# A two-layer hybrid trunk: three more engines keep the program's order

## The chip, the cores and the metric

The kernel runs on one core of a Trainium2 chip. The metric is the device time of the program in microseconds (us), the median of 3 runs of the kernel before: 746.13 (745.88 to 746.42).

## The reference

The kernel computes a decoder trunk of two layers over a residual stream of 1024 features, 16 learned meta tokens and then 256 real ones. All data are float32.

- Layer 0 normalises (RMSNorm) and multiplies by one input matrix whose columns are split over two mixers. *Sparse attention*, 8 heads of 64: a small indexer scores every key for every query, the 64 best keys are kept (the meta tokens always), then softmax with a relative-position bias. *Retention*, 4 heads (128 for query and key, 256 for value): rotary positions, scores times a decay, a group norm and a swish gate. Both outputs go through one output matrix and are added to the stream.
- Layer 1 has *stick-breaking attention*, 16 heads of 64: with z the score of an earlier key, its weight is exp(log sigmoid(z) + sum of log sigmoid(-z') over the keys between). An output matrix and the addition follow.
- After each mixer comes a gated MLP of 2816 hidden features: up and gate projections, a causal convolution of width 3 over the gate, silu(gate) times up, a down projection, the addition. A last RMSNorm ends it.

```
z = einsum(q, k) * scale
log_1m = where(mask, log_sigmoid(-z), 0)
rest = cumsum(log_1m, reverse) - log_1m
a = where(mask, exp(log_sigmoid(z) + rest), 0)
out = einsum(a, v)
```

## The kernel before, in words

**Data.** Features lie on the partitions, the 272 tokens on the free axis. Every weight matrix is cut into 128 x 128 tiles, read once and in one order, as a stream of chunks of 16 tiles (1 MB). `Stream` (from L89) holds three such chunks (`raw`), and splits each half chunk of eight tiles into two parts in the type fp32r: ScalarE copies `hi` (L122), VectorE subtracts it from `raw` to get `lo` (L126). Activations are split likewise (`xh` and `xl`, `ah` and `al`, `oh` and `ol`). A product is then three matmuls: high by high, low by high, high by low (L197 to L199).

**Order on TensorE.** `project` runs jobs one after the other; a job is a group of 8 to 22 tile products into one PSUM bank, and an evacuation on the other engines. `get`, called before each tile, makes `lo` two halves ahead of the tile in use and `hi` three halves ahead; four halves are kept. Everything else that TensorE does (scores, transposes, attention products) stands in coroutines that `Sched.tick` moves on by one step, every four tile products (L199 and after). A coroutine issues its step's instructions on all engines and then yields a number of ticks, which are fixed by hand (`D0` to `D6`, `AV`, `RS`, `PT`, `TK`, `VT`, `VC`).

**Order on the other engines.** The context is opened with a planner that simulates a time line and orders each engine's instructions by it. L76 takes TensorE out of that: it keeps the program's order throughout. The start (from L338) and the first norm are inside narrower blocks that pin ScalarE and VectorE, in the first also GpSimd. Everywhere else the planner orders ScalarE, VectorE, GpSimd and SyncE, and SyncE issues the weight loads.

**Layer 0's mixer.** `indexer` fills `sc` and `drop` with zeros, adds the relu scores, runs six rounds of max and match_replace (L451, L453) and writes `drop` (L459). `dsa` takes pairs of heads: `bm` = `drop` minus bias on GpSimd (L524), scores (L530, L531), minimum on VectorE (L534), exponential on ScalarE (L537), normalise (L543, L545), transposes (L551 to L554), their copies `ptk` (ScalarE) and `ptm` (VectorE, L557), products with the values (L566 to L571). `dsa_meta` does the meta tokens' own rows: a memset of `pf` (L581), the scores of 16 x 16 (L587) with an evacuation into `pf`, softmax, transposes, `pts` (L606), products (L612). `ev_rot` evacuates a rotary query or key into `qb` or `kb`, with the last addition on GpSimd (L642). `ret` transposes values (L671 to L673), scales and centres them as `vb` (L680, L687), and multiplies them with the scores (L696 to L698). There are three banks of pool "a" for all this, and three for projections.

**Feed-forward.** `ev_g` evacuates a gate group and starts `c` on ScalarE (L911); a tick later come two VectorE passes and silu, and `ev_u` gives `u`. 22 pairs of groups in each layer.

**Layer 1's stick-breaking.** Jobs run q, k for eight pairs of heads, and v three pairs later. `ev_q` makes `qc` and its parts, `ev_k` the parts `kd` and `kl` of the keys. `stick` then goes in steps: scores (L1069, L1070) and their copies `zs`; absolute value (L1075), exponential (L1077), logarithm (L1078); max-add into `sp` (L85) and masks on GpSimd (L1014); addition of 16 rows, parts `sh` (L1086) and `sl` (L82); the cumulative sums as products (L1093 to L1101), each subtracted from `zs`; exponential (L1104) and masks; products with `vt` (L1117 to L1121), `oh` (L1122) and `ol`. `v_t` transposes `vv` and copies it into `vt` (L1055). Two buffers of most tiles, four banks of pool "a", one of "o".

Of the kernel before, what the change touches and what calls it, by code (L numbers as in the profile page):

```python
# [65 lines left out]
def trunk(ctx, tc, hT, wp, gains, gng, convw, convb, relb, oneh, cosT, sinT, decay, gfin, out):  # L66
# [6 lines left out]
    tmp = ctx.enter_context(tc.tile_pool(name="tmp", bufs=2))  # L73
    pp = ctx.enter_context(tc.tile_pool(name="pp", bufs=3, space=PSUM))
    dram = ctx.enter_context(tc.tile_pool(name="dram", bufs=1, space=DRAM))
    ctx.enter_context(tc.manual_schedule(engines={mybir.EngineType.PE}))  # L76

    def log_exp():
        tc.keep_in_program_order(S.preload_act_table_set("natural_log_exp_and_others"))
# [1157 lines left out]
```

## Time and profile before

| | us |
|---|---|
| median of 3 runs | 746.13 (745.88 to 746.42) |
| profiled execution | 745.54 |
| its span, first to last instruction | 743.5 |
| mean granted TensorE clock, share of full speed | 0.997 |
| TensorE busy in the span | 726.9 |
| VectorE, ScalarE, GpSimd busy | 538.4, 420.8, 87.8 |

One profiled execution is read; its span leaves out 2.0 us around the program's own instructions. The chain that ended last, followed back from the last instruction, gives 88% of the span to TensorE, 5% to VectorE, 2% each to ScalarE and GpSimd. To place the stages in time: layer 0's first `c` of the feed-forward (L911) starts at 224.2 us, the first `qs` copy of the stick-breaking layer (L1024) at 424.0, its last `oh` (L1122) at 527.0, and layer 1's last `c` at 670.6.

### The profile page before, as it was taken

What the parts mean: (1) busy time and instruction counts of PE and PEld (TensorE: products, weight loads), DVE (VectorE), ACT (ScalarE), POOL (GpSimd) and SP (SyncE); (2) the same over time, 40 slices, a digit from 0 to 9 for tenths busy, and PEclk for the clock granted to TensorE, in tenths of its full rate; (3) what the DMA queues carried; (4) which work ended last, traced back from release to release, by engine and by line L of the source; (5) the groups of instructions that cost most, each with busy time, mean ns of one, the idle gap of its engine ahead of it and who ended that gap; (6) DMA issues with size and microseconds to landing.
All of it is one profiled execution on the core that took longest, in us unless ns stands there. A gap on an engine that the chain in (4) does not pass through costs nothing.

```text
span 743.5 us, 14066 instructions
## 1 busy us (share of the span) xinstructions
PE 726.9 (98%) x5706; PEld 701.9 (94%) x5706; DVE 538.4 (72%) x981; ACT 420.8 (57%) x706; POOL 87.8 (12%) x157
## 2 busy tenths in 40 slices
PE   8999899999999999999999999999999999999996
PEld 7889798989999999999999999999999999998895
DVE  6888666758768788877556678878688878885542
ACT  6456646568446555555434598776446555554532
POOL 2114312100000000000000266342000000000000
PEclk9999999999999999999999999999999999999998
DMA  8663333425545555555445443333345555555521
GB/s 308 211 211 126 120 119 114 168 73 170 174 169 175 174 177 182 180 181 180 171 170 171 152 155 112 132 133 114 114 171 204 198 197 170 177 199 173 188 86 57
DMA packets 20408, 120.01 MB, mean 161 GB/s; under 512 B 2648, under 2 KB 4376, under 8 KB 6904
## 3 DMA queue, kind: packets, MB, share of 16 engines
q1 hardware_dynamic: 19392, 116.89, 46.1%
q0 software_dynamic: 528, 1.50, 0.6%
q8 instruction: 45, 0.74, 0.4%
q10 hardware_dynamic: 424, 0.73, 0.3%
q14 instruction: 19, 0.16, 0.1%
HBM read 117.85 MB, written 1.25 MB: 160 GB/s over the span
## 4 chain that ended last, share of the span: by engine, by line
PE 88%; DVE 5%; ACT 2%; issue 2%; POOL 2%; DMA 1%; SPq 0%; DVEq 0%; POOLq 0%; ACTq 0%
PE bank L197 24%; PE bank L198 24%; PE bank L199 24%; PE bank L814 3%; PE bank L812 3%; PE bank L813 3%; DVE lo L126 2%; ACT hi L122 1%; DMA raw<-in_wp 1%; PE bank L1093 1%; PE bank L1117 1%; POOL bm L524 1%; DVE tk L453 1%; PE bank L804 0%; PE bank L1069 0%
## 5 line engine op out<-in xcount | busy, mean ns | idle before, releaser
L197 PE MATMUL bank<-xh,hi 128*128 128x272 f32 (+2 forms) x1224 | 356.9, 292 | 0.3 <-ACT hi L122 0.3
L122 ACT ACTIVATE hi<-raw 128x1024 fp32r<-128x1024 f32 (+1 forms) x220 | 229.7, 1047 | 218.9 <-PE bank L198 128.6
L199 PE MATMUL bank<-xh,lo 128*128 128x272 f32 (+2 forms) x1224 | 350.5, 286 | 0.5 <-DVE lo L126 0.4
L198 PE MATMUL bank<-xl,hi 128*128 128x272 f32 (+2 forms) x1224 | 350.1, 286 | 0.3 <-DVE xl L85 0.3
L126 DVE TENSOR_TENSOR lo<-raw,hi 128x1024 fp32r<-128x1024 f32 (+1 forms) x220 | 266.8, 1214 | 102.6 <-ACT hi L122 99.4
L197 PEld LDWEIGHTS bank<-xh,hi 128*128 128x128 f32 x1224 | 230.5, 188 | 5.0 <-issue 3.5
L198 PEld LDWEIGHTS bank<-xl,hi 128*128 128x128 f32 x1224 | 230.5, 188 | 1.4 <-DVE xl L85 0.9
L199 PEld LDWEIGHTS bank<-xh,lo 128*128 128x128 f32 x1224 | 230.5, 188 | 1.2 <-DVE lo L126 1.2
L197 PE MATMUL bank<-ah,hi 128*128 128x272 f32 x176 | 50.7, 288 | 0.0
L199 PE MATMUL bank<-ah,lo 128*128 128x272 f32 x176 | 50.6, 288 | 0.0
L198 PE MATMUL bank<-al,hi 128*128 128x272 f32 x176 | 50.6, 287 | 0.0
L85 DVE SCALAR_TENSOR_TENSOR c<-gb,cw,c 128x272 f32<-128x272 f32 (+1 forms) x88 | 42.6, 486 | 0.0
L812 PE MATMUL bank<-hi,ah 128*128 128x512 f32 (+1 forms) x110 | 38.3, 348 | 0.0
L814 PE MATMUL bank<-lo,ah 128*128 128x512 f32 (+1 forms) x110 | 38.2, 347 | 0.0
L813 PE MATMUL bank<-hi,al 128*128 128x512 f32 (+1 forms) x110 | 38.1, 346 | 0.0
L197 PEld LDWEIGHTS bank<-ah,hi 128*128 128x128 f32 x176 | 33.1, 188 | 0.0
L198 PEld LDWEIGHTS bank<-al,hi 128*128 128x128 f32 x176 | 33.1, 188 | 0.0
L199 PEld LDWEIGHTS bank<-ah,lo 128*128 128x128 f32 x176 | 33.1, 188 | 0.0
L933 ACT CAST ah<-c 128x272 fp32r<-128x272 f32 (+1 forms) x44 | 17.6, 403 | 26.2 <-DVE c L82 26.2
L82 DVE TENSOR_TENSOR gb<-bank,rstd 128x272 f32<-128x272 f32 (+1 forms) x44 | 19.1, 434 | 13.5 <-PE bank L199 13.3
L197 PE MATMUL bank<-oh__202,hi 128*128 128x272 f32 x96 | 27.8, 290 | 0.0
L199 PE MATMUL bank<-oh__202,lo 128*128 128x272 f32 x96 | 27.8, 289 | 0.0
(275 smaller groups left out, 997.8 us busy)
## 6 DMA issues: line engine op xcount, KB each, us to landing
raw<-in_wp SPq DMA_DIRECT2D x105, 1024.0 KB, 4.9
raw<-in_wp SPq DMA_DIRECT2D x4, 512.0 KB, 7.0
raw<-in_wp SPq DMA_DIRECT2D x6, 256.0 KB, 5.8
bias<-btab SPq DMA_DIRECT2D x8, 136.0 KB, 3.0
dec<-in_decay POOLq DMA_DIRECT2D x4, 216.0 KB, 5.4
h<-in_hT SPq DMA_DIRECT2D x3, 272.0 KB, 6.3
gf<-in_gfin POOLq DMA_DIRECT2D x1, 512.0 KB, 4.3
out_y<-fo ACTq DMA_DIRECT2D x2, 256.0 KB, 2.8
```

The costliest lines, as they stand in the source:

```text
L82: V.tensor_tensor(out=out, in0=a, in1=b, op=op)
L85: V.scalar_tensor_tensor(out=out, in0=a, scalar=s, in1=b, op0=op0, op1=op1)
L122: S.activation(out=self.half[h][0][:, a * 128:b * 128], in_=self.src(h, a, b), func=AF.Copy)
L126: V.tensor_tensor(out=lo[:, a * 128:b * 128], in0=self.src(h, a, b), in1=hi[:, a * 128:b * 128].bitcast(F32), op=ALU.subtract)
L197: PE.matmul(self.ps, wh, xh, start=k == 0, stop=False)
L198: PE.matmul(self.ps, wh, xl, start=False, stop=False)
L199: PE.matmul(self.ps, wl, xh, start=False, stop=k == n - 1)
L453: V.match_replace(out=nx, in_to_replace=m8, in_values=cur[b], imm_value=FILL)
L812: PE.matmul(ps[:, :n], xd[k][0][:, t], wh, start=False, stop=False)
L813: PE.matmul(ps[:, :n], xd[k][1][:, t], wh, start=False, stop=False)
L814: PE.matmul(ps[:, :n], xd[k][0][:, t], wl, start=False, stop=k == FT - 1)
L933: S.copy(out=ah[:, f], in_=c)
```

## The change

The one call that pins TensorE names three more engines. From there on ScalarE, VectorE and GpSimd issue their instructions in the order in which the program's text, with its coroutines, calls them. SyncE is not named: the planner still orders its loads.

```diff
-    ctx.enter_context(tc.manual_schedule(engines={mybir.EngineType.PE}))
+    ctx.enter_context(tc.manual_schedule(engines={mybir.EngineType.PE, mybir.EngineType.Activation, mybir.EngineType.DVE,
+                                                   mybir.EngineType.Pool}))
```

## Rows read from the trace of the kernel before

**Rows 1.** Page, busy time: us, share of the span, instructions.

```profile
PE 726.9 (98%) x5706; PEld 701.9 (94%) x5706; DVE 538.4 (72%) x981; ACT 420.8 (57%) x706; POOL 87.8 (12%) x157
```

**Rows 2.** TensorE's waits: line <- releaser, us in total, times, longest.

```profile
PE bank L673 <- DVE ptm L557: 4.2, 3, 1.4
...
PE bank L566 <- DVE ptm L557: 1.1, 1, 1.1
...
PE bank L696 <- DVE vb L687: 0.6, 1, 0.6
```

**Rows 3.** Windows, feed-forward and stick-breaking: length, busy us, clock, DMA share, GB/s.

```profile
core 0: us, PE busy (x) PEld busy (x) DVE busy (x) ACT busy (x) POOL busy (x), PEclk, DMA share, GB/s
300.00:320.00 20.00, 20.00 (x161) 20.00 (x160) 16.05 (x28) 10.33 (x16) 0.00 (x0) 1.00 0.52 163
480.00:500.00 20.00, 20.00 (x173) 19.55 (x173) 14.85 (x26) 15.79 (x30) 7.75 (x14) 1.00 0.49 159
```

**Rows 4.** Timeline of VectorE near 90 us: start, duration, instruction, idle before.

```profile
90.18 1.22 DVE L126 TENSOR_TENSOR lo<-raw,hi 128x1024 fp32r<-128x1024 f32 x1 [0.52 <-ACT hi L122]
91.32 0.47 DVE L557 COPY ptm<-bank 64x128 f32<-64x128 f32 x2
```

**Rows 5.** Timelines of GpSimd and VectorE in the mixer.

```profile
4.11 0.30 POOL L581 MEMSET pf<- 16x256 f32 x1
...
62.34 4.62 POOL L524 TENSOR_TENSOR bm<-drop,bias 128x144 f32<-128x144 f32 x4 [6.87 <-DVE drop L459]
...
137.69 0.76 POOL L642 TENSOR_TENSOR qb<-qb,ru 128x272 f32<-128x272 f32 x1 [7.02 <-DVE ru L82]
...
140.88 1.80 POOL L642 TENSOR_TENSOR kb<-kb,ru 128x272 f32<-128x272 f32 x1 [2.42 <-DVE ru L82]
...
141.97 0.34 DVE L82 TENSOR_TENSOR pf<-bank,bias 16x64 f32<-16x64 f32 x2
```

**Rows 6.** Timelines of VectorE and ScalarE, start of layer 0's feed-forward.

```profile
217.57 1.22 DVE L126 TENSOR_TENSOR lo<-raw,hi 128x1024 fp32r<-128x1024 f32 x1
...
224.19 0.60 ACT L911 ACTIVATE c<-gb,cb,cw 128x272 f32<-128x272 f32 x1
```

**Rows 7.** Groups by form, 420 to 530 us: count, busy us, mean ns, idle before.

```profile
L126 DVE TENSOR_TENSOR lo<-raw,hi 128x1024 fp32r<-128x1024 f32 x25 | 31.3, 1255 | 6.9 <-ACT hi L122 6.8
...
L122 ACT ACTIVATE hi<-raw 128x1024 fp32r<-128x1024 f32 x26 | 27.3, 1053 | 11.5 <-PE bank L198 11.4
...
L82 DVE TENSOR_TENSOR sl<-sp,sh 128x836 fp32r<-128x836 f32 x8 | 8.5, 1059 | 1.1 <-ACT sh L1086 0.9
...
L1078 ACT ACTIVATE sp<-sp,one 128x836 f32<-128x836 f32 x8 | 7.9, 988 | 0.1
...
L1086 ACT CAST sh<-sp 128x836 fp32r<-128x836 f32 x8 | 7.1, 884 | 0.8 <-DVE sp L82 0.8
...
L1035 ACT CAST kd<-bank 64x272 fp32r<-64x272 f32 x16 | 6.0, 375 | 1.8 <-DVE kl L82 1.5
...
L1075 DVE TENSOR_SCALAR sp<-zs 128x836 int32<-128x836 int32 x8 | 4.9, 608 | 1.4 <-ACT zs L1073 1.3
```

**Rows 8.** Timeline of GpSimd near 487 us.

```profile
486.86 0.91 POOL L1014 TENSOR_SCALAR_AFFINE_SELECT zs<-zs 128x228 f32<-128x228 f32 x3 [1.67 <-ACT zs L1104]
487.72 1.98 POOL L1014 TENSOR_SCALAR_AFFINE_SELECT sp<-sp 128x228 f32<-128x228 f32 x3
```

**Rows 9.** Chain of waits at L1093: start, duration, what.

```profile
442.92 0.28 PE bank L1093 x2
...
470.75 0.28 PE bank L1093 x2
...
483.69 0.28 PE bank L1093 x2
...
496.63 0.29 PE bank L1093 x2
```

**Rows 10.** Page, DMA issues: count, KB each, median us from issue to landing.

```profile
raw<-in_wp SPq DMA_DIRECT2D x105, 1024.0 KB, 4.9
```

## The prediction

> **What bounds the kernel now.** I read the busy table first: TensorE is busy 726.9 of the 743.5 us span, its weight loads 94%, VectorE 72%, ScalarE 57%, GpSimd 12% [rows 1]. TensorE's order is the program's already, so it can gain only where it still waits. The list of its waits says how little that is: the bank that L673 wants, held until `ptm` is copied, 4.2 us in three waits, then pieces of about 1 us [rows 2]. The windows say what cover the other engines have: in the feed-forward TensorE works 20.00 of 20 us beside a VectorE with 16.05 and a ScalarE with 10.33; in the stick-breaking stretch again 20.00, beside 14.85 and 15.79 and a GpSimd with 7.75 [rows 3]. Full TensorE and three engines at 40 to 80%: what matters is whether their new order is a chain that fits into TensorE's period, not how busy they are.
>
> All sums are made against the profiled execution, 743.5 us of span and 2.0 around it, 745.5, 0.6 under the median of 746.13; I add the 0.6 at the end.
>
> **Part 1: waits that go.** Around 90 us VectorE takes a `lo` (L126, 1.22 us from 90.18) and only then the two `ptm` copies (from 91.32) [rows 4]. `ptm` stands behind the transposes in the program and the `lo` behind it, so in program order the copy runs about 1.6 us earlier, when its transposes are through. All three waits at L673 and the one at L566 are of this kind: 4.2 + 1.1. L696's 0.6 shrinks to about 0.1, because `vb` is no longer behind other work, and 0.2 comes from small ones. Sum: -5.9, with 4 and 6 as its ends.
>
> **Part 2: the mixer's first and last head pair.** In program order VectorE runs each top-k round's max and replace back to back, with the norm's reciprocal chain in front of them; by my walk through the list `drop` ends near 68.0 us in place of 62.2. The four `bm` on GpSimd that follow it took 4.62 us at 62.34 [rows 5]; they are issued one tick ahead of their scores, about 1.5 us. The chain `drop`, `bm`, minimum, exponential, normalise then reaches the transposes at 75.9 to 76.8, where TensorE stands at about 74.2: +2.2 (1.7 to 2.6).
> The meta rows' `pf` memset is the second. It ran at 4.11 us, far ahead [rows 5]; in the program it comes after head 3's `kb` addition (1.80 us from 140.88) and the fourth pair's four `bm` (about 2.7). VectorE's `pf` evacuation (141.97 [rows 5]) therefore waits until about 145.6, and behind it on VectorE stand the minima that free the three score banks: TensorE's second half of L530 waits about 3.1 us, and the meta rows' own transposes then 1.0. The ends are 1.2 (a `kb` at 0.76, as `qb` took [rows 5], and `bm` to match) and 4.6. Three `vb` lose 0.1 each. Sum of part 2: +2.2 + 3.1 + 1.0 + 0.3 = +6.6.
>
> **Part 3: where stages meet.** Stream issues `lo` two halves ahead, inside `get`, after evacuations that the program places before it. At the start of layer 0's feed-forward the `lo` that ran at 217.57 [rows 6] now stands behind `c` of ScalarE (0.60 [rows 6]), two VectorE passes of 0.5 and the `u` evacuation, and is done near 226.7 where TensorE wants it at 225.8: +0.9. The same at the start of layer 1's feed-forward, +0.9, after the stick-breaking layer +0.4, at the mixer's out-projection +0.3. Sum +2.5, ends 0 (if `lo` keeps its lead) and 4.
> Inside the feed-forwards I count nothing: VectorE needs about 5 us for each pair of groups against some 6 us of TensorE (16.05 of 20 [rows 3]), and `lo` is ready some 4 us early. If that cover went, each of the 44 pairs could cost up to 0.3.
> A raw buffer comes free later, by about 3 us, because `lo` reads it later; it lands 4.9 after its issue [rows 10] and by my walk is read some 12 us after, so this costs nothing.
>
> **Part 4: the stick-breaking layer.** In the planned order ScalarE, VectorE and GpSimd take whatever is ready. In program order one pair of heads becomes a single chain that passes from engine to engine, since each piece stands behind the one before it on its own queue: absolute value 0.61; four ScalarE passes over the pair's 836 columns (exponential, logarithm, weights' exponential, `sh`), 0.88 to 0.99, together 3.66; between them two `kd` casts at 0.375, one `hi` 1.05, one `oh` and one `ol`, 0.4 each; the max-add and `sl` on VectorE, 1.05 and 1.06; the masks on GpSimd, 0.91 [rows 7, 8]; the 16-row addition 0.18; then `vv` and `qc`, about 0.43 each (nearest row: `kd`), with a `lo` of 1.26 behind each, and three subtractions after L1093, 1.3 [rows 7]. Sum 14.8; instructions that follow each other on one engine start 0.08 earlier than the durations say (90.18 + 1.22 against 91.32 [rows 4]), so 14.5. TensorE's own period is 12.94, from 483.69 to 496.63 at L1093 [rows 9].
> Early pairs have no `vv`, `ol`, `oh` and one `lo`: about 12.0. TensorE comes by at 442.92 and 470.75 three pairs later, 9.28 each [rows 9]: +2.7 per pair, of which the delays between a pair's pieces take up the first. By my walk the L1093 of the eight pairs start 0.3, 0.8, 4.4, 4.6, 5.2, 6.6, 7.8 and 12.2 later. From the fifth on this is 14.5 - 12.94 less some slack, about +1.3 each; the last step, +4.4, is `vt` copies of the last pairs behind max-add, `ol` and a `lo` on VectorE. Sum +12.2. If all of it is hidden it is 0 (TensorE's waits here are too small to give more); with masks at 1.98, as at 487.72 [rows 8], it is 20.
> I take 12.2 because rows 7 are this stretch's own durations; the walk from them is the uncertain thing, not the prices.
>
> Here a rule speaks against the change, seen first in the rows: the same three-block mask took 0.91 us at 486.86 and 1.98 at 487.72, with VectorE at work [rows 8]; `qb` 0.76 and `kb` 1.80 [rows 5]. The Trainium skill, SBUF — State Buffer, section "SBUF: two separate sides", says that VectorE and GpSimd share one pair of ports as an exclusive lock, and that the one that comes second blocks for the other's whole instruction. By that rule a GpSimd piece in each chain may double; as a time this is rival 3.
>
> **Sum.** -5.9 + 6.6 + 2.5 + 12.2 = +15.4: 760.9, and 761.5 on the median's basis.
>
> **Rivals.** *Rival 1, the chains are covered (the other side, faster).* It decides at 1.6 us per pair: if so much of the 14.5 runs beside other pieces of the chain, a pair fits in 12.94 and part 4 is about 0; if the same slack covers parts 2 and 3, -5.9 remains with about 1 back: 741. For it: no wait of TensorE's is above 1.4 us now, and ScalarE and VectorE have 4 to 5 of 20 us free [rows 2, 3]. Against it: that free time is waiting for each other, which an order by readiness fills and a fixed order doesn't. The Trainium skill, Perfetto Trace Analysis, section "Identifying the Most-Contended Engine", judges VectorE and ScalarE by occupancy and has the busiest engine bind; by that TensorE stays the bound and the change gives this rival's time. The trace agrees for the kernel before.
> *Rival 2, only the mixer and the seams.* Part 4 stays under the delays between a pair's pieces for all but the last: -5.9 + 6.6 + 2.5 + 0 to 4 = +3 to +7, 749 to 753; with the small ends of parts 2 and 3 (+3 and 0) 743 to 747.
> *Rival 3, GpSimd at its long durations.* Each mask 1.07 longer in eight chains, +8.5, and up to 3 in the mixer, where `bm` and `kb` follow VectorE: 770 to 775.
> *Rival 4, it doesn't do what it says:* loads are planned anew or the order stays, 746. Nothing in the trace speaks for it but that SyncE is left out of the set.
>
> **How the numbers follow.** Forecast 0.62 (753 to 768); rival 1 0.15; rival 2 0.12, of it a third within the uncertainty; rival 3 0.09; rival 4 0.02. 0.2%, about 1.5 us, is what a measurement can tell from no change. Faster 0.16 (rival 1 and a little of rival 2), same 0.06, slower 0.78. The range 747 to 775 holds the forecast, nearly all of rival 3 and most of rival 2, and leaves out rival 1. Cases of both signs share the chance, but the likeliest one's own range is 753 to 768.
>
> **What would show it.** Right: no wait at L673 and L566 for `ptm`; new waits of TensorE at L551 near 75 us, at L530 near 143 to 147, and at L1069, L1093 and L1117 in the stick-breaking stretch; L1093's starts 14.3 to 14.6 apart where they are 12.94 now; feed-forward windows that keep TensorE at 20.00 of 20. Wrong: a period that stays 12.94 with waits under 1 us (rival 1 or 2), masks at 1.9 throughout (rival 3), new waits inside the feed-forward, which I count at nothing, or a wait for raw loads.

## The result, and the profile after

The changed kernel takes 771.06 us (770.23 to 773.7, 4 runs) against 746.0 (745.62 to 746.42, 4 runs): a ratio of 1.0342, 95% interval 1.0329 to 1.0354. The forecast was 761.5, slower; the loss is 25 us where 15.4 were forecast. Line numbers of the changed kernel are one higher than before, and those of the experiments' kernels by a few more; the tiles' names tell which line is meant.

The page of the kernel after, busy time and the chain that ended last, answers to [rows 1]. Before, the chain had 88% on TensorE and 5%, 2% and 2% on the others.

```profile
PE 736.7 (96%) x5706; PEld 707.1 (92%) x5706; DVE 537.1 (70%) x981; ACT 424.0 (55%) x705; POOL 76.3 (10%) x157
...
PE 74%; DVE 13%; ACT 7%; POOL 3%; issue 2%; DMA 1%; SPq 0%; DVEq 0%; POOLq 0%; ACTq 0%
```

VectorE and ScalarE do about the same work (537.1 us for 538.4, and 424.0 for 420.8), at lower shares of a longer span: it hardly got more expensive, it got later. TensorE's waits answer to [rows 2]: `ptm` is nearly gone, and these, among others, are new or larger.

```profile
PE bank L200 <- DVE lo L127: 4.4, 9, 0.9
PE bank L1070 <- DVE zs L83: 3.9, 2, 2.4
PE bank L1118 <- DVE vt L1056: 3.7, 2, 2.1
PE bank L1094 <- DVE sl L83: 2.8, 5, 0.7
PE bank L531 <- DVE pf L83: 2.3, 1, 2.3
PE bank L1094 <- ACT sh L1087: 1.4, 2, 0.8
PE bank L199 <- DVE ol L83: 1.3, 1, 1.3
...
PE bank L552 <- ACT pr L544: 1.1, 1, 1.1
```

TensorE has the same 5706 instructions in the same order in both kernels, so the start of the n-th can be subtracted: how far the changed kernel is behind at that point. I call it the lag. Its growth by stretch, in the one profiled execution of each kernel, is counted from 25 us on. By then the executions differ from the one before by 0.25 to 0.9 us already, 0.45 in a kernel that is unchanged up to 424 us, and that is left out:

| kernel | layer 0's mixer | start of its feed-forward | layer 1's mixer | start of its feed-forward | median, us |
|---|---|---|---|---|---|
| the change | 2.7 | 1.2 | 20.1 | 1.3 | 771.06 |
| forecast | 1.0 | 0.9 | 12.6 | 0.9 | 761.5 |

Within the feed-forwards and in the tail the lag stays flat (4.24 from 236 to 425 us), as forecast. Four fifths of the loss arise in layer 1's mixer.

**The chain, where it is periodic.** VectorE's `vv` comes once in a pair of heads. Its starts in the timeline of the changed kernel:

```profile
483.50 0.43 DVE L83 TENSOR_TENSOR vv<-bank,rstd 128x272 f32<-128x272 f32 x1
...
498.65 0.43 DVE L83 TENSOR_TENSOR vv<-bank,rstd 128x272 f32<-128x272 f32 x1
...
513.80 0.43 DVE L83 TENSOR_TENSOR vv<-bank,rstd 128x272 f32<-128x272 f32 x1
```

They are 15.15 apart, twice, where TensorE's period before was 12.94 [rows 9]. The chain of waits of the changed kernel between two of them (start, duration, what) shows who hands on to whom:

```profile
500.55 1.13 DVE lo L127
501.68 1.06 DVE zs L83 x3
502.75 0.72 DVE sp L1076
...
503.49 0.91 ACT sp L1078
...
504.42 0.99 ACT sp L1079
505.41 0.79 ACT zs L1105
506.20 0.28 ACT kd L1036
...
506.51 0.45 DVE kl L83
...
506.97 0.39 ACT kd L1036
...
507.39 0.44 DVE kl L83
...
507.87 1.39 DVE lo L127
...
509.28 0.43 DVE ol L83
509.71 0.95 DVE sp L86
...
510.78 0.92 POOL sp L1015 x3
...
511.93 0.90 ACT sh L1087
```

No TensorE instruction stands in it: for a whole round the three engines wait only for each other. Of the 15.15 us some 9.5 are VectorE's pieces (3.65 of them three `lo`), 4.3 ScalarE's and 0.9 GpSimd's.

**The clock.** A loss that the prediction did not have: behind some of the new waits TensorE's granted clock falls to half. The windows behind the wait at L531 (length; busy us of PE, PEld, DVE, ACT, POOL; clock; DMA), of the changed kernel:

```profile
142.00:146.00 4.00, 2.16 (x7) 1.46 (x8) 1.57 (x11) 1.31 (x5) 1.88 (x5) 0.77 0.55 229
146.00:150.00 4.00, 4.00 (x27) 3.92 (x26) 3.83 (x16) 3.54 (x11) 0.00 (x0) 0.80 0.00 0
```

A clock of 0.50 is the level of 1.2 GHz, 1.00 that of 2.4; a mean between them has part of its window at either. The same happens from about 454 to 458 and 498 to 504 us, with waits of 2.5 and twice 0.95 ahead.

### The profile page after: what moved, and what is told of

It reads as the page before. It is cut to its first block, busy times and chain, and to the rows that moved or that the text cites. A ratio compares the mean times of both kernels' runs of the same rounds, so it can differ in the third digit from the quotient of the medians.

```text
span 768.5 us, 14037 instructions
## 1 busy us (share of the span) xinstructions
PE 736.7 (96%) x5706; PEld 707.1 (92%) x5706; DVE 537.1 (70%) x981; ACT 424.0 (55%) x705; POOL 76.3 (10%) x157
## 4 chain that ended last, share of the span: by engine, by line
PE 74%; DVE 13%; ACT 7%; POOL 3%; issue 2%; DMA 1%; SPq 0%; DVEq 0%; POOLq 0%; ACTq 0%
PE bank L198 20%; PE bank L200 20%; PE bank L199 20%; DVE lo L127 4%; PE bank L815 3%; PE bank L813 3%; PE bank L814 3%; POOL sp L1015 1%; ACT sh L1087 1%; ACT sp L1079 1%; ACT sp L1078 1%; DVE zs L83 1%; DMA raw<-in_wp 1%; POOL bm L525 1%; DVE sp L86 1%
## 5 line engine op out<-in xcount | busy, mean ns | idle before, releaser
L912 ACT ACTIVATE c<-gb,cb,cw 128x272 f32<-128x272 f32 (+1 forms) x44 | 26.8, 610 | 45.7 <-DVE gb L83 45.7
L918 ACT ACTIVATE c<-c 128x272 f32<-128x272 f32 (+1 forms) x44 | 18.7, 425 | 34.3 <-DVE c L86 34.2
```

Source lines behind the costliest of these rows:

```text
L912: S.activation(out=c, in_=g[:, 2:], func=AF.Identity, scale=cw[:, 2, f:f + 1], bias=cb[:, f:f + 1])
L918: S.activation(out=c, in_=c, func=AF.Silu)
```

## The experiments

The theory at the start: in program order one pair's pieces form a chain longer than TensorE's period, and TensorE's other losses are single late pieces. First, where does the loss arise, and does it add up?

**Only the stick-breaking layer pinned.**

```diff
+    pin.enter_context(tc.manual_schedule(engines=THREE))
     with ExitStack() as m1:
...
+    pin.close()
     ffn(1, nm, META, None)
```

> The three engines are pinned in layer 1's stick-breaking layer alone (with its output projection); elsewhere the planner orders them as before. Chain theory: TensorE's lag on the kernel before grows from 4.2 us at the layer's start to 24.4 at its end in the changed kernel, and nothing of that is inherited from the mixer, so this run takes 746.1 + 20 = 766 (764.5 to 767). Rival, inheritance: part of the lag is loads or splits of weights that the pinned feed-forward hands over late; then this run is under 762.

766.61 us, ratio 1.0274 (1.0258 to 1.0289). The layer's own growth of lag is 20.2, with `vv` again 15.16 apart.

**All but that layer pinned**, the complement: the three are pinned from the start, released before the layer and pinned again after it.

> The complement of the first run: pinned everywhere but in layer 1's stick-breaking layer. Chain theory: the lag left is 3.1 at the end of the mixer, 1.1 to 1.2 at the start of each feed-forward, 5.4 in sum: 751.5 (750.5 to 753). The two runs' changes add up to that of the full change (25). Rival, inheritance: over 755.

750.69, ratio 1.0057 (1.0040 to 1.0073). 20.4 + 4.5 = 24.9 of 25.1: the stretches do not inherit from each other. Rival inheritance falls.

**Pinned in two windows of layer 0's mixer**, meant to keep the gains alone.

```diff
-        project(jobs)
+        project(jobs[:9])
+        pin.enter_context(tc.manual_schedule(engines=THREE))
+        project(jobs[9:21])
+        pin.close()
+        project(jobs[21:25])
+        pin.enter_context(tc.manual_schedule(engines=THREE))
+        project(jobs[25:])
+        pin.close()
```

> Pinned only in two windows of layer 0's mixer: its projections 10 to 21, which begin after the top-k chain and end before the meta tokens' own rows, and the last three. Step theory: the waits for ptm at L566 (1.1) and L673 (three of 1.15) go and nothing new comes: 746.1 - 4.5 = 741.6 (740.8 to 742.6). Rival: the planner, free outside the windows, moves other work into the new gaps or loses at a window's edge: 744 to 748.

746.92, ratio 1.0013 (1.0003 to 1.0022): a miss. Two of the four `ptm` waits went. The other two lay behind the windows' ends (one grew from 1.38 to 1.77), and the second window held what it should have left out: GpSimd's queue in this kernel, by timeline, is the changed kernel's again.

```profile
138.80 1.80 POOL L645 TENSOR_TENSOR kb<-kb,ru 128x272 f32<-128x272 f32 x1 [1.81 <-DVE ru L85]
140.56 2.38 POOL L527 TENSOR_TENSOR bm<-drop,bias 128x144 f32<-128x144 f32 x4
142.88 0.30 POOL L584 MEMSET pf<- 16x256 f32 x1
```

**The memset of `pf` moved to the mixer's set-up**, all else as in the change.

```diff
+        pf = mx.tile([16, 8, 32], F32, name="pf")
+        G.memset(pf, 0.0)
         def dsa_meta():
-            pf = mx.tile([16, 8, 32], F32, name="pf")
-            G.memset(pf, 0.0)
```

> All three pinned as in the change, but the memset of pf is issued when the mixer is set up, not inside the meta rows' step. Wait theory: TensorE's 2.3 us wait at L531 and its short ones around it go, 3.5 in sum: 767.5. Wait and clock theory: after that wait the granted clock is 0.54 to 0.60 from 144 to 148 us, which costs 1.3 more; without the wait the clock stays 1.00: 771.1 - 4.8 = 766.3. Rival: the chain through kb and bm, not the memset, holds pf: under 1 us gained.

767.53, ratio 1.0289 (1.0272 to 1.0307), 3.5 less than the change. The wait at L531 is gone, 3.3 with the short ones around it, and the clock reads 1.00 throughout 138 to 162. The time is the wait theory's, but for another reason: what is late next is the meta rows' own transposes, a wait that the prediction priced at 1.0 and that the change itself did not show. From this kernel's waits:

```profile
PE bank L607 <- DVE pf L83: 1.5, 1, 1.5
```

**One engine at a time.** Beside TensorE only VectorE, only ScalarE, only GpSimd is named, as here:

```diff
-    ctx.enter_context(tc.manual_schedule(engines={mybir.EngineType.PE}))
+    ctx.enter_context(tc.manual_schedule(engines={mybir.EngineType.PE, mybir.EngineType.DVE}))
```

> TensorE and VectorE pinned, ScalarE and GpSimd left to the planner. Chain theory: the 15.2 us per pair of heads is one chain only because all three engines are held; with ScalarE and GpSimd free, their pieces (weights' exponential, casts, masks) move out of the way of VectorE's, so the stick-breaking layer costs under half of its 20: 6 to 10. The mixer keeps the gains of ptm (-4.6) and the late drop (+1.8), and loses the wait for pf; the seams, which are VectorE's lo, stay (+3): 746.1 + 8 = 754 (750 to 757). Rival, VectorE theory: VectorE carries the lo passes and all late pieces, its order alone makes the loss: 764 to 770.

> TensorE and ScalarE pinned. Chain theory: VectorE and GpSimd are planned around ScalarE's fixed order; ptm waits stay as before (no gain), the stick-breaking layer costs 1 to 4: 749 (747 to 751). Rival, ScalarE theory: its exponentials and logarithms in the program's order make the chain: over 756.

> TensorE and GpSimd pinned. Chain theory: GpSimd's order costs only what stands behind kb and bm, the memset of pf, about 1 to 4 with the clock: 748 (746 to 751). Rival, GpSimd theory: its masks behind the qs subtractions (2.0 to 2.1 us) make the early waits of the stick-breaking layer: 752 to 757. If the three single pins add up to about 25, there is no common chain.

| pinned beside TensorE | mixer 0 | ffn 0 | mixer 1 | ffn 1 | median, us | ratio, 95% interval |
|---|---|---|---|---|---|---|
| all three | 2.7 | 1.2 | 20.1 | 1.3 | 771.06 | 1.0342 (1.0329 to 1.0354) |
| VectorE | 4.5 | 1.7 | 16.4 | 1.8 | 769.54 | 1.0314 (1.0298 to 1.0329) |
| ScalarE | -4.1 | 0.0 | 7.9 | 0.1 | 747.81 | 1.0024 (1.0014 to 1.0034) |
| GpSimd | 2.1 | 0.0 | 2.2 | 0.1 | 750.28 | 1.0056 (1.0041 to 1.0071) |

The chain theory's forecast for VectorE, 754, is wrong by 15, and the rival's 764 to 770 is right: VectorE's order alone costs 23.4 of the 25 us. ScalarE's time lies in its forecast by luck: no gain in the mixer and 1 to 4 lost in layer 1 were expected, 4.1 were gained and 7.9 lost. GpSimd's lies at the upper end of its range. The three losses add up to 29 us, in layer 1 to 26.5, where the three engines together cost 25 and 20.1. A sum of about 25 was to mean that there is no common chain. The sum is larger, so the losses overlap: much of what three fixed orders cost is there with one of them.

Slow clock is part of these readings. While TensorE works without a wait, the lag grows by 1.5 and 3.1 us in VectorE's run (clock 0.63 from 468 to 472 us, 0.59 and 0.56 from 540 to 548) and by 2.6 in ScalarE's (0.50 and 0.63 from 450 to 457), whose profiled execution, 749.34, is one of its longest. Without such growth, some 3 in the changed kernel, layer 1's 20.1, 16.4, 7.9 and 2.2 would be about 17, 12, 5 and 2, an estimate from these lags.

Where in the layer the loss arises is told by the lag at each pair's first L1093, from the layer's start:

| pinned | pair 1 | 2 | 3 | 4 | 5 | 6 | 7 | 8 | end |
|---|---|---|---|---|---|---|---|---|---|
| forecast | 0.3 | 0.8 | 4.4 | 4.6 | 5.2 | 6.6 | 7.8 | 12.2 | 12.6 |
| all three | 1.1 | 5.1 | 9.1 | 9.1 | 10.4 | 13.0 | 14.6 | 19.6 | 20.1 |
| VectorE | 1.1 | 4.0 | 8.5 | 8.5 | 7.9 | 9.2 | 9.7 | 12.9 | 16.4 |
| ScalarE | 0.0 | 1.6 | 5.5 | 6.5 | 6.8 | 6.8 | 6.8 | 8.0 | 7.9 |
| GpSimd | 0.0 | 0.0 | 0.0 | 0.0 | 0.0 | 0.7 | 1.3 | 2.3 | 2.2 |

From the fourth pair to the seventh the three together lose 5.6, VectorE alone 1.2, ScalarE 0.3, GpSimd 1.3. There the chain needs more than one engine held, as the theory has it, and VectorE's `vv` come 14.40, 13.47 and 13.63 apart in its own run (from 484.26 on). In the first three pairs VectorE's order alone costs 8.5 of the change's 9.1, and ScalarE's alone 5.5; from the seventh pair to the end VectorE's costs 6.7, more than the change's 5.5, with 3.1 of clock in it. So the chain that needs all three is shown for the middle of the layer only.

**VectorE pinned in two windows of the mixer**, repairing the miss above: projections 9 to 22, and the last value projection with the first two of the gate; only VectorE, so that the memset stays early.

```diff
+        dve.enter_context(tc.manual_schedule(engines={mybir.EngineType.DVE}))
+        project(jobs[9:23])
+        dve.close()
```

> VectorE alone pinned, in two windows of layer 0's mixer: projections 9 to 22, and the last rotary-value projection with the first two of the gate; meta rows, GpSimd and ScalarE are left to the planner. In the order of the build, ptm stands ahead of the lo that it followed, four times, and pf's memset stays early. Step theory: 1.13 + 3 x 1.15 = 4.6 gained and nothing lost: 741.6 (740.9 to 742.6), faster than both kernels. Rival: a lo that now waits for ptm is late for TensorE, or the planner's new order outside loses: 744 to 748.

742.71, ratio 0.9955 (0.9940 to 0.9969), just above the forecast range. It gains, but L673 gives 0.77 each, not 1.15: VectorE's `ptm` (90.20, idle 2.07 before it) now waits for `ptk`, and that stands behind a `hi` that ScalarE's planned order puts first. Timeline of ScalarE in this kernel:

```profile
88.75 1.06 ACT L125 ACTIVATE hi<-raw 128x1024 fp32r<-128x1024 f32 x1 [1.31 <-PE bank L201]
89.71 0.84 ACT L559 COPY ptk<-bank 128x384 f32<-128x384 f32 x2
```

**Waits filled.** Matmuls that nothing reads are put into two of the waits that had slow clock behind them.

```diff
+                if j == 1 and hh == 1:
+                    fill(bank(pools["o"]), 16)
...
+                    if j == 4 and hh == 0:
+                        fill(lb, 7)
```

> The changed kernel with matmuls added that nothing reads: 16 (128 x 128 by 256) ahead of the second half of the scores of the second pair of heads, where TensorE waited 2.5 us, and twice 7 ahead of the fifth pair's first two cumulative sums, where it waited 0.95 and 0.95. They fill waits and shorten none. Clock theory: the granted clock, 0.50 to 0.70 from 454 to 458 us and 0.50 to 0.86 from 498 to 504, stays at 1.00 and the 1.4 and 1.6 us that the slow stretches cost come back: 771.1 - 3 = 768. Rival, waits alone: the time goes into the waits that follow, 771 (within 0.6); if the added matmuls delay the next work, 772 to 774.

773.35 (770.18 to 775.25), ratio 1.0360 (1.0335 to 1.0386), no better than the change: the clock theory's 768 is not reached. The clock did as expected at the two places and then fell at two others, and in the mixer it stayed at half for longer than in the change (0.50 from 144 to 150 us). So the run doesn't settle what filling a wait is worth. Windows of this kernel, columns as above:

```profile
454.00:458.00 4.00, 2.97 (x25) 2.98 (x26) 2.92 (x5) 3.48 (x5) 2.55 (x4) 1.00 0.60 246
498.00:502.00 4.00, 3.89 (x30) 3.52 (x29) 3.04 (x6) 3.42 (x9) 0.00 (x0) 1.00 0.41 172
468.00:472.00 4.00, 4.00 (x23) 3.92 (x22) 1.97 (x4) 2.62 (x7) 1.76 (x6) 0.62 0.10 39
544.00:548.00 4.00, 2.72 (x19) 2.18 (x18) 2.09 (x5) 0.38 (x1) 0.00 (x0) 0.77 0.48 143
```

What the clock costs is told better by kernels that share the mixer's order. The same wait at L531 has 0.77 and 0.80 behind it in the change (above). In the run with all but the stick-breaking layer pinned the windows are these:

```profile
142.00:146.00 4.00, 2.30 (x7) 1.60 (x8) 1.44 (x9) 1.18 (x5) 1.73 (x4) 0.63 0.54 227
146.00:150.00 4.00, 4.00 (x18) 3.77 (x18) 3.29 (x14) 3.67 (x11) 0.00 (x0) 0.52 0.00 0
```

And in the next experiment's first kernel, the changed one with a mask done twice in layer 1, these:

```profile
142.00:146.00 4.00, 1.71 (x11) 1.34 (x11) 1.62 (x11) 1.36 (x6) 2.33 (x5) 1.00 0.58 231
146.00:150.00 4.00, 3.98 (x33) 3.68 (x32) 3.83 (x14) 3.75 (x13) 0.00 (x0) 1.00 0.00 0
```

Their lag over the mixer is 2.7, 4.0 and 1.2. Same instructions, and the same wait of 2.29 us: the slow stretch comes in one execution and not in another, and is worth up to 2.8 us. How much of the 25 is clock in all is not settled; in the profiled execution the three stretches, read as growth of lag while TensorE works without a wait, are about 1, 1.4 and 1.6.

**The mask on `sp` done twice**, in the changed kernel and in the kernel before: the second time changes no value.

```diff
             mask(sp, 0.0)
+            mask(sp, 0.0)
```

> The changed kernel, with the mask on sp (0.92 us on GpSimd for each pair of heads) done twice; the second changes nothing. Chain theory: that piece is on the chain of every pair, so L1093 of each comes 0.92 later than the one before: 5.5 to 7.4 in sum, 777.5 (776 to 779). Rival, room: the program's order loses by late VectorE pieces at a few places only, and GpSimd, busy 1.7 of 5 us, has room: 771 to 773.

> The same doubled mask in the kernel before. Chain theory: in the planned order the piece is hidden behind other work, 0 to 1 later: 746.5 (745.8 to 747.5). Rival: the mask is on a chain in the planned order too: over 749.

In the changed kernel: 779.58, ratio 1.0448 (1.0434 to 1.0463), just above the chain theory's range; the rival, room on GpSimd, is refuted. The cleanest reading is again VectorE's `vv`, and GpSimd's doubled mask beside it:

```profile
485.87 0.43 DVE L83 TENSOR_TENSOR vv<-bank,rstd 128x272 f32<-128x272 f32 x1
...
501.89 0.43 DVE L83 TENSOR_TENSOR vv<-bank,rstd 128x272 f32<-128x272 f32 x1
...
517.90 0.43 DVE L83 TENSOR_TENSOR vv<-bank,rstd 128x272 f32<-128x272 f32 x1
...
514.02 1.77 POOL L1015 TENSOR_SCALAR_AFFINE_SELECT sp<-sp 128x228 f32<-128x228 f32 x6 [2.60 <-DVE sp L86]
```

16.01 and 16.02 apart, 0.86 more, for a mask that is 0.86 longer (1.77 against 0.91): a piece on GpSimd, an engine busy a tenth of the time, goes into the period one to one. The exponentials of the first and the eighth pair are 93.54 us apart in the changed kernel (440.07 to 533.61) and 99.54 here (439.02 to 538.56): seven times 0.86. The rest of the 8.5 goes with a lower clock (0.983 in the mean against 0.991); it is not read apart.
In the kernel before: 751.85, ratio 1.0078 (1.0064 to 1.0092). I had expected almost nothing, and the rival is right. The lag is 4.1 by the second pair and 5.5 at the end, so in the planned order too the mask is on a chain in the layer's first two pairs, and only from there mostly hidden (1.4 more for six pairs); about 1.5 of the 4.1 is clock, 0.72 from 445 to 450 us. Its waits:

```profile
PE bank L1094 <- ACT sh L1087: 1.9, 1, 1.9
PE bank L1094 <- DVE sl L82: 1.7, 2, 0.9
```

**What the runs point to.** ScalarE's order is worth 4.1 in the mixer, VectorE's 1.1 at L566, and neither belongs in layer 1.

```diff
+    act.enter_context(tc.manual_schedule(engines={mybir.EngineType.Activation}))
...
-        project(jobs)
+        project(jobs[:9])
+        dve.enter_context(tc.manual_schedule(engines={mybir.EngineType.DVE}))
+        project(jobs[9:12])
+        dve.close()
+        project(jobs[12:])
...
+    act.close()
     with ExitStack() as m1:
```

> The kernel before with ScalarE pinned up to the end of layer 0's feed-forward, and VectorE pinned during projections 9 to 11 of the mixer; the stick-breaking layer is planned as before. From the single pins: ScalarE's order takes 0.7 at L696 and three times 1.15 at L673, VectorE's window 1.1 at L566: 746.1 - 5.2 = 740.9 (740.2 to 741.8). Rival: the planner, which starts the stick-breaking layer from another simulated state, orders it worse: 743 to 748.

740.82 (740.72 to 740.95), ratio 0.9930 (0.9918 to 0.9943): faster than both and as forecast. The lag falls by 4.7 in the mixer, where 5.2 were added up: VectorE's window takes 0.5 of the 1.1 at L566. The median gives 5.2 because the profiled execution before, 745.54, lies 0.5 under the median of its runs here. The waits for `ptm` that are left:

```profile
PE bank L676 <- DVE ptm L560: 0.7, 3, 0.2
...
PE bank L569 <- DVE ptm L560: 0.5, 1, 0.5
```

## Why the prediction was right, and where its sizes were not

The sign and the places held, and the mechanism held where the stick-breaking layer is periodic; the loss came out 1.6 times as large, and three quarters of what was missing is part 4. The time lies above the 753 to 768 that I gave the forecast itself. It is inside 747 to 775 because that range was drawn to hold rival 3 too, whose mechanism did not occur. That the number lies in the range is luck.

**Part 1** forecast -5.9; the lag falls by 0.72 at L696, 1.13 at L566 and three times 1.15 at L673: -5.3, right. The reason given was half of it. I said VectorE's `lo` stood ahead of `ptm`; so it did, but `ptm` also waits for `ptk`, and ScalarE's planned order had `hi` ahead of that. With ScalarE alone pinned, VectorE still in planned order, `lo` has its `hi` sooner and `ptm` is early near 90 us:

```profile
88.13 1.23 DVE L126 TENSOR_TENSOR lo<-raw,hi 128x1024 fp32r<-128x1024 f32 x1 [0.64 <-ACT hi L122]
89.27 0.43 DVE L85 SCALAR_TENSOR_TENSOR aq<-bank,rstd 128x272 f32<-128x272 f32 x1
89.94 0.28 DVE L557 COPY ptm<-bank 64x128 f32<-64x128 f32 x1 [0.24 <-ACT ptk L556]
```

**Part 2.** The late `drop` forecast +2.2, measured 1.75. The meta rows forecast 3.1 for the wait at L531 and 1.0 for their transposes; measured 3.3 for the first with its short ones, nothing for the second, and in this execution about 1 of clock. The path was the one named: VectorE's `pf` evacuation waits for the memset behind `kb` and `bm`, which answers to [rows 5].

```profile
143.57 0.34 DVE L83 TENSOR_TENSOR pf<-bank,bias 16x64 f32<-16x64 f32 x2 [3.22 <-POOL pf L582]
```

**Part 3** forecast 0.9 at each feed-forward and measured 1.2 and 1.3; the mixer's gate and out-projection, which I had at 0.3, took 1.1 (0.71 and 0.38), both as waits for a `lo`. The feed-forwards cost nothing, as said.

**Part 4 is the term that was mis-sized**: 12.2, and the layer took 19.6 to its last pair. Its 7.4 too little is made of three pieces. In the first three pairs I gave 4.4 and 9.1 was lost: I let the delays between a pair's pieces absorb the first 3 us. In the lag the 9.1 are a `lo` at the layer's start (1.1), two waits at L1070 for banks that the subtractions `zs` free (2.5 and 1.7), one at L1118 for `vt` (2.2), and 1.5 of clock. The early chain itself, 12.0 in the forecast, runs at 11.5 to 11.8 between exponentials (440.07, 451.60, 463.39), so its price was right; but by its first exponential it is 3.1 behind already (440.07 less the 4.24 of lag, against 432.69), which is the cushion that I had counted on. Also, GpSimd takes the `qs` subtractions first, which I had left out, and the mask stands behind them; that this costs anything by itself is not shown, since GpSimd's order alone loses nothing in these pairs.

```profile
442.38 2.00 POOL L1026 TENSOR_TENSOR qs<-qc,qs 64x258 fp32r<-64x258 f32 x2 [4.11 <-ACT qs L1025]
444.46 0.91 POOL L1015 TENSOR_SCALAR_AFFINE_SELECT sp<-sp 128x228 f32<-128x228 f32 x3
```

In the middle I had 14.5 against 12.94; it is 15.15. The chain above has two `kl` on VectorE (0.45 and 0.44), between the two `kd` casts and behind them, and a third `lo` (1.39) that I did not count; the `hi` and the `oh` that I did count (1.05 and 0.4) run beside it. So 5.6 was lost over three pairs, not 3.2. The last pair, 4.4 forecast, took 5.0, but only 1.6 of it is the wait for `vt` that I named; most of the rest are waits for `sl` (0.95), `oh` (0.6) and `ol` (1.55). Of the layer's lag some 3 is the clock, in the stretches at 454 and 498, which lies inside these three pieces.

Part 4's mechanism was also drawn too wide. I had one chain that passes through three engines because all three keep the program's order. That is so from the fourth pair to the seventh. In the other pairs VectorE's order by itself, with the two others planned around it, is late by about as much as all three.

**The rivals.** Rival 1 (covered chains, faster) is refuted by the period of 15.15, rival 2 by the layer's 20, and rival 4 (it doesn't do what it says) by both. Rival 3 named 770 to 775 and the time falls into it, but its mechanism is refuted: in the changed kernel every mask on `sp` is short, 8 of each form with means of 383, 406 and 213 ns, 1.0 in sum, and GpSimd's busy time fell from 87.8 to 76.3. The Trainium skill, SBUF — State Buffer, section "SBUF: two separate sides", has a GpSimd instruction and a VectorE instruction that needs the pair of ports they share exclude each other; no run here contradicts it, and the trace shows why it did not bite on the masks: in a chain VectorE waits while GpSimd runs (2.34 us idle ahead of the 16-row addition). In the mixer some pieces did lengthen, `qb` from 1.28 to 1.76 us in the mean. One group of masks and that addition, in the changed kernel:

```profile
L1015 POOL TENSOR_SCALAR_AFFINE_SELECT sp<-sp 128x228 f32<-128x228 f32 x8 | 3.1, 383 | 19.0 <-DVE sp L86 18.9
...
445.40 0.18 DVE L83 TENSOR_TENSOR sp<-sp 16x32 f32<-16x32 f32 x1 [2.34 <-POOL sp L1015]
```

The Trainium skill, Perfetto Trace Analysis, section "Identifying the Most-Contended Engine", would have one optimize the engine with the highest occupancy. In layer 1 the measurement differs: over the span TensorE has the highest share, 96%, but a chain over VectorE at 70, ScalarE at 55 and GpSimd at 10% set the period, and a piece on GpSimd lengthened it one to one.

## What to carry to other kernels

An engine's queue is a promise about order: where one pair's pieces pass several times between three engines, a fixed order can turn the sum of all their durations into the period, whatever each engine's busy share is, and one engine's fixed order can be enough to make most of the loss. Add up that round before pinning, with every piece that sits between two of its links, and compare it with the period of the engine to be kept busy; do not count on the delays between pieces to absorb the first of it. Then pin by stretch and by engine: here ScalarE pinned through layer 0, with VectorE over three of its projections, is worth -5.2 us, and all three pinned in layer 1's mixer cost 20. Not tried were other delays between the steps (`D0` to `D6`) or fewer `lo` passes on VectorE; whether any fixed order loses here, or only the one that this program's text gives, stays open.

## What was not expected of the hardware

TensorE's clock. After a wait of 2.29 us the granted clock read 0.52 to 0.80 in the windows behind it in two executions and 1.00 in a third of the same instructions, and the time of the changed kernel goes with it: its four runs took 770.23, 770.49, 771.63 and 773.7 at mean clocks of 0.991, 0.991, 0.989 and 0.985, while the kernel that beats both stayed within 0.23 us at 0.997 to 0.998. Waits do not always make a kernel that unsteady: with only the stick-breaking layer pinned, four runs lay within 0.7 us at 0.991 to 0.994.
